# Delta-rule scan: longer gaps between some of its steps, a tile taken later, and the output projection begun beside the last scan but one

## The chip, the cores and the metric

The kernel runs on one core of a Trainium2 chip. The metric is the device time of one execution in microseconds (us). The core has a matrix engine (TensorE, PE in the profile), a vector engine (VectorE, DVE), a scalar engine (ScalarE, ACT), GpSimd (POOL) and a queue for transfers (SyncE, SP). Each takes its own instructions in order, and they wait for one another by semaphores.

## The reference

Two layers over 768 tokens (512 of one group, 256 of another) with 1024 features: a Fourier-style layer, then a bidirectional gated delta rule; each is followed by a SwiGLU mixer. The change lies in the second layer's mixer, which for 8 heads of width 128 computes:

```python
def gdn_mixer(h, w_in, conv_w, a_log, dt_bias, norm_g, w_out):
    proj = h @ w_in
    qkv = jax.nn.silu(centred_depthwise_conv(proj[..., :GDN_QKV_DIM], conv_w))
    z = proj[..., GDN_QKV_DIM:GDN_QKV_DIM + GDN_V_DIM]
    ...
    q = l2norm(q) * (GDN_HEAD_DIM ** -0.5)
    k = l2norm(k)
    ...
    o_fwd = gated_delta_chunked(q, k, v, g[:, :, 0], beta[:, :, 0])
    o_bwd = gated_delta_chunked(q[:, ::-1], ..., g[:, ::-1, 1], beta[:, ::-1, 1])[:, ::-1]
    o = o_fwd + o_bwd
    o = o * lax.rsqrt(jnp.mean(o * o, axis=-1, keepdims=True) + EPS) * norm_g * jax.nn.silu(z)
    return o.reshape(bsz, s, GDN_V_DIM) @ w_out
```

Within a chunk the rule needs the inverse of a unit triangular matrix; between chunks a state is carried on.

## The kernel before

Data lie feature by token. The 768 tokens are two segments (512 and 256) for long products and six chunks of 128 for the delta rule. A long product is made of split operands, a high and a low half each: per k-step and segment three matmuls, hh with wh, hl with wh, hh with wl (`passes`, all recorded at L128; the output is a PSUM bank named pr).

For each head, `prepare(h)` issues four such projections of eight k-steps: k, q, v and z. The first three pass through `conv_block` (conv on VectorE, L948, silu with L886 on VectorE and three steps on ScalarE). Beside the projections stand the steps of the delta rule, by a planner: every k-step calls `tick`, which moves a modelled clock, `line["now"]`, on and issues each step that is due, right behind that k-step (`run_next`). PLACES are the due times of the preparing steps (norm of k, products of k and q, transposes of v) after the head's base; SCAN is that of the start of `scan(h)`, which so stands beside the projections of head h + 1; HOPS are the gaps between the steps of the scan, which is a generator that yields the next gap. A Tile scheduler then orders each engine's instructions; what it decides is shown below by rows of the built programs.

`solve` (L1054 to L1071) inverts blocks of 16 by a chain of small VectorE steps between two passes through DRAM and yields cc. `invert` doubles the blocks at levels 16, 32 and 64: r (a masked cc, one half on POOL, one on VectorE, L1088), then transposes `ident,cc` (L1095), masked to t (VectorE, L1097), products `t,am` (am is the level's part of the matrix, masked on POOL), copied to t again (ScalarE, L1109; called zz here), products `r,t`, subtracted from cc (VectorE, L1119) or, at the last level, copied into rr (ScalarE, L1122, L1123). Four steps of the scan proper follow, over both directions at once: `st,kT`, xx (VectorE, L1155), `xx,rr` (`vk,rr` in the first), yk and yy (ScalarE), `yk,kk`, st (VectorE, L1172).

The scan's end: products `pm,yy` and `qd,st`, copied to ob (ScalarE, L1186); two squares on ScalarE (L1191, L1192), summed on POOL (L1193); a hop; products `yy,ones`; logarithm and exponential (L1199, L1200), two VectorE steps (L1201, L1202), and the head's gated output goes to DRAM (ogd, SP, L1204). The buffer rr of `invert` is also the one that L1196 takes at the scan's end.

The output projection reads heads 0 to 6 back from ogd into two buffers "wa" in turn (SP, L1216) and splits each into hh (ScalarE, L195) and hl (VectorE, L196), which overwrite the operands of the projections. Seven blocks of it run beside the last scan, number 7; block 7 and head 7's part come after. `residual` (VectorE, L473) adds a block to x. The products have three PSUM banks: two for segments of 512 (pr0) and one for 256 (pr1).

Of the kernel before, what the change touches and what calls it, by code (L numbers as in the profile page):

```python
# [12 lines left out]
F32 = mybir.dt.float32  # L13
# [7 lines left out]
P = 128  # L21
# [27 lines left out]
LANES = NT * P // BASE  # L49
LSTEP = BASE * (P + 1)  # L50
NEGBIG = -1e30
HOPS = (1150.0, 1300.0, 1500.0, 1400.0, 1300.0, 2080.0, 1150.0, 2700.0)
PLACES = (16100.0, 20200.0, 22900.0, 29400.0, 36200.0)
SCAN = 34100.0

_TAB = {}

# [48 lines left out]
def encoder_kernel(  # L106
# [53 lines left out]
    def load_block(w2d, k0, kc, m0):  # L160
        stg = fetch(w2d, k0, kc, m0)
        ah, al = [], []
        step = kc if kc <= HK else (kc + 1) // 2
        for a in range(0, kc, step):
            n = min(step, kc - a)
            wh, wl = split_w(stg[:, a : a + n])
            ah += [wh[:, k] for k in range(n)]
            al += [wl[:, k] for k in range(n)]
        return ah, al
# [612 lines left out]
    with ExitStack() as gs:  # L782
# [16 lines left out]
        def work(name="wa", bufs=2):  # L799
            return ga.tile([P, T + 2], F32, name=name, bufs=bufs)  # L800
# [99 lines left out]
        def run_next():  # L900
            t, _, fn = heapq.heappop(line["due"])
            with tc.issue_after(line["ins"]):
                fn()
# [175 lines left out]
        def invert(src):  # L1079

            cc = src["cc"]
            rr = gp.tile([P, 2, NT, P], F32, name="rr")
            halves = range(0, NT, NB)
            for lv in LEVELS:
                am = src["am"]
                r2 = gp.tile([P, NT, P], F32, name="r2")
                for b0 in halves:
                    (G if b0 in R2G else V).tensor_tensor(r2[:, b0 : b0 + NB], cc[:, b0 : b0 + NB], mask(f"B{lv}", NB), ALU.mult)  # L1088
                if lv != LEVELS[0]:
                    yield HOPS[0]  # L1090
                t1 = {}
                for b0 in halves:
                    pt = psm.tile([P, 512], F32, name="sm")
                    for i in range(NB):
                        nc.tensor.transpose(pt[:, i * P : (i + 1) * P], cc[:, b0 + i], ident)  # L1095
                    t1[b0] = gp.tile([P, NB, P], F32, name="t1", bufs=3)
                    V.tensor_tensor(t1[b0], tiles6(pt[:, : NB * P]), mask(f"A{lv}", NB), ALU.mult)  # L1097
                if lv == LEVELS[-1]:
                    for d in range(2):
                        G.affine_select(rr[:, d], cc, pattern=[[0, NT], [1 - 2 * d, P]], compare_op=ALU.is_ge, fill=0.0,  # L1100
                                        base=0, channel_multiplier=2 * d - 1)
                yield HOPS[1]
                zz = {}
                for b0 in halves:
                    pt = psm.tile([P, 512], F32, name="sm")
                    for i in range(NB):
                        mm(pt[:, i * P : (i + 1) * P], am[:, b0 + i], t1[b0][:, i])
                    zz[b0] = gp.tile([P, NB, P], F32, name="t1", bufs=3)
                    A_.copy(zz[b0], tiles6(pt[:, : NB * P]))  # L1109
                if lv != LEVELS[-1]:  # L1110
                    siblings(src, 2 * lv)
                yield HOPS[2]
                for b0 in halves:
                    cm = cc[:, b0 : b0 + NB]
                    pt = psm.tile([P, 512], F32, name="sm")
                    for i in range(NB):
                        mm(pt[:, i * P : (i + 1) * P], zz[b0][:, i], r2[:, b0 + i])
                    if lv != LEVELS[-1]:
                        V.tensor_tensor(cm, cm, tiles6(pt[:, : NB * P]), ALU.subtract)  # L1119
                    else:  # L1120
                        hp = P // 2
                        A_.copy(rr[:hp, 0, b0 : b0 + NB, hp:], tiles6(pt[:hp, : NB * P])[:, :, hp:])  # L1122
                        A_.copy(rr[hp:, 1, b0 : b0 + NB, :hp], tiles6(pt[hp:, : NB * P])[:, :, :hp])  # L1123
            return rr

        def scan(h, src):
# [11 lines left out]
            for stp in range(4):  # L1138
# [17 lines left out]
                    xin = lambda i: xx[:, i]  # L1156
                else:
                    xin = lambda i: vk[:, live[i][1]]
                yield HOPS[4]
                py = group(lambda d, j: rr[:, d, j], xin, len(live))  # L1160
                yk = gp.tile([P, 4, P], F32, name="yk") if more else None
                for i, (d, j) in enumerate(live[:more]):
# [46 lines left out]
        for h in range(H):  # L1209
            prepare(h)  # L1210

        while H - 2 not in scanned:
            run_next()
        for h in range(H - 1):
            ob = work()[:, :T]
            nc.sync.dma_start(ob, ogd[h])  # L1216
            split_to(hh[h], hl[h], ob)

        xs = [ga.tile(pad_shape, F32, name="pad"), *(ga.tile(head_shape, F32, name=n, bufs=b) for n, b in (("qT", 2), ("vT", 1))),
              work("we"), work("we"), work(), work()]  # L1220
        xs = [x[:, :T] for x in xs]
        for m in range(KC - 1):
            nc.sync.dma_start(xs[m], xd[m])
            po = product(ppr, load_block(gdn_w_out[0], 0, H - 1, m * P), hh, hl, H - 1, tick)
            residual(xs[m], po, GATE[2], m)
        drain()
# [123 lines left out]
```

## Time and profile before

| what | value |
|---|---|
| runs shown | 2956.52, 1903.44, 1901.87 us, median 1903.44 |
| profiled execution | 1905.38 us |
| its span, first to last instruction | 1903.7 us |
| mean granted TensorE clock | 0.989 |
| stretch of the six scans beside whole projections | 853 to 1233 us |
| the last head's projections, output projection, last scan | 1233 to 1345 us |

A wait in the profile is idle time of an engine ahead of an instruction, put down to what released it. In rows of the timeline the first column is the start in us from the span's start, the second the duration, and the bracket at the end the idle time with its releaser. In rows of stretches the columns are the busy times of the engines in it, then the granted clock, the share of the DMA engines, and GB/s. In groups by line the last columns are the busy time in us and the mean in ns, then idle time ahead.

### The profile page before, as it was taken

What the parts mean: (1) busy time and instruction counts of PE and PEld (TensorE: products, weight loads), DVE (VectorE), ACT (ScalarE), POOL (GpSimd) and SP (SyncE); (2) the same over time, 40 slices, a digit from 0 to 9 for tenths busy, and PEclk for the clock granted to TensorE, in tenths of its full rate; (3) what the DMA queues carried; (4) which work ended last, traced back from release to release, by engine and by line L of the source; (5) the groups of instructions that cost most, each with busy time, mean ns of one, the idle gap of its engine ahead of it and who ended that gap; (6) DMA issues with size and microseconds to landing.
All of it is one profiled execution on the core that took longest, in us unless ns stands there. A gap on an engine that the chain in (4) does not pass through costs nothing. (4 is left out here: it accounts for less than half of the span.)

```text
span 1903.7 us, 29939 instructions
## 1 busy us (share of the span) xinstructions
PE 1800.2 (95%) x11305; PEld 1641.0 (86%) x11305; DVE 1419.6 (75%) x2415; ACT 974.5 (51%) x1860; POOL 539.8 (28%) x436
## 2 busy tenths in 40 slices
PE   7898999999999998999999999989889999999998
PEld 6587889999999986888888888778789999999997
DVE  4636777767786777897787787783768888889875
ACT  3625544444454535856566556642654554555543
POOL 1403132333333320123213212321343334443431
PEclk9999999999999999999999999999999999999999
DMA  8742344343434354322212222141203222222211
GB/s 272 242 171 67 111 132 130 109 140 112 154 111 155 111 160 142 115 51 64 65 53 65 68 64 57 57 151 41 77 23 89 77 79 67 67 67 80 77 45 67
DMA packets 221546, 189.72 MB, mean 100 GB/s; under 512 B 19152, under 2 KB 199513, under 8 KB 221401
## 3 DMA queue, kind: packets, MB, share of 16 engines
q1 hardware_dynamic: 220992, 187.66, 32.2%
q8 instruction: 89, 1.46, 0.3%
q14 instruction: 56, 0.46, 0.1%
q10 hardware_dynamic: 409, 0.15, 0.0%
HBM read 174.36 MB, written 13.42 MB: 99 GB/s over the span
## 5 line engine op out<-in xcount | busy, mean ns | idle before, releaser
L128 PE MATMUL pr<-hh,wh 128*128 128x384 f32 (+2 forms) x1520 | 520.7, 346 | 15.0 <-ACT cs__676 L736 5.6
L128 PE MATMUL pr<-hl,wh 128*128 128x384 f32 (+2 forms) x1520 | 519.0, 342 | 6.9 <-DVE hl L196 6.6
L128 PE MATMUL pr<-hh,wl 128*128 128x384 f32 (+2 forms) x1520 | 517.8, 341 | 1.0 <-DVE wl L148 1.0
L147 ACT CAST wh<-stg 128x512 fp32r<-128x512 f32 (+1 forms) x376 | 226.2, 609 | 369.8 <-PE pr L128 254.5
L148 DVE TENSOR_TENSOR wl<-stg,wh 128x512 fp32r<-128x512 f32 (+1 forms) x376 | 290.9, 779 | 108.4 <-ACT wh L147 107.3
L128 PEld LDWEIGHTS pr<-hh,wh 128*128 128x128 f32 x1520 | 286.2, 189 | 39.2 <-ACT cs__676 L736 6.1
L128 PEld LDWEIGHTS pr<-hl,wh 128*128 128x128 f32 x1520 | 287.5, 189 | 25.6 <-DVE hl L196 8.6
L128 PEld LDWEIGHTS pr<-hh,wl 128*128 128x128 f32 x1520 | 286.8, 189 | 18.4 <-DVE wl L148 1.8
L128 PE MATMUL pr<-g,wh 128*128 128x384 f32 (+2 forms) x1072 | 274.1, 337 | 8.7 <-DVE x L552 8.7
L128 PEld LDWEIGHTS pr<-g,wh 128*128 128x128 f32 x1072 | 192.7, 188 | 13.4 <-DVE x L552 11.6
L128 PE MATMUL pr<-eh,wh 128*128 128x384 f32 x536 | 184.2, 347 | 13.3 <-ACT eh L195 9.2
L128 PE MATMUL pr<-el,wh 128*128 128x384 f32 x536 | 182.6, 341 | 0.4 <-DVE el L196 0.4
L128 PE MATMUL pr<-eh,wl 128*128 128x384 f32 x536 | 182.5, 340 | 0.0
L128 PE MATMUL pr<-g,wl 128*128 128x384 f32 (+2 forms) x536 | 180.3, 336 | 0.0
L383 POOL TENSOR_TENSOR s<-stg 128x512 f32<-128x512 f32 x42 | 60.1, 1432 | 402.2 <-DMA stg<-in_ffn_w_gu_dram 360.8
L128 PEld LDWEIGHTS pr<-eh,wh 128*128 128x128 f32 x536 | 102.5, 192 | 22.4 <-ACT eh L195 10.1
L517 DVE TENSOR_TENSOR wl<-stg,wh 128x512 fp32r<-128x512 f32 x108 | 88.2, 818 | 34.1 <-ACT wh L516 33.3
L948 DVE SCALAR_TENSOR_TENSOR wa<-pad,cwT,wa 128x770 f32<-128x770 f32 x96 | 108.9, 1134 | 4.6 <-ACT wa L945 3.3
L516 ACT CAST wh<-stg 128x512 fp32r<-128x512 f32 x108 | 66.9, 621 | 80.5 <-PE pr L128 63.2
L128 PEld LDWEIGHTS pr<-el,wh 128*128 128x128 f32 x536 | 102.3, 191 | 1.4 <-DVE el L196 1.3
L128 PEld LDWEIGHTS pr<-eh,wl 128*128 128x128 f32 x536 | 102.3, 191 | 0.0
L128 PEld LDWEIGHTS pr<-g,wl 128*128 128x128 f32 x536 | 100.6, 188 | 0.7
(370 smaller groups left out, 3172.9 us busy)
## 6 DMA issues: line engine op xcount, KB each, us to landing
stg<-in_ffn_w_gu_dram SPq DMA_DIRECT2D x88, 512.0 KB, 4.1
stg<-in_ada_w_dram SPq DMA_DIRECT2D x56, 512.0 KB, 5.0
at<-in_ada_w_dram SPq DMA_DIRECT2D x40, 512.0 KB, 4.8
stg<-in_ffn_w_down_dram SPq DMA_DIRECT2D x36, 512.0 KB, 3.7
stg<-in_gdn_w_in_dram SPq DMA_DIRECT2D x33, 512.0 KB, 4.2
stg<-in_final_ada_w_dram SPq DMA_DIRECT2D x16, 512.0 KB, 6.1
raw<-gcd SPq DMA_DIRECT2D x8, 768.0 KB, 4.0
stg<-in_fnet_w_dram SPq DMA_DIRECT2D x8, 512.0 KB, 7.7
```

The source lines that it names most:

```text
L128: return nc.tensor.matmul(out, lhsT, rhs, start=start, stop=stop, **kw)
L147: A_.copy(wh[:, :n], src)
L148: V.tensor_tensor(wl[:, :n], src, wh[:, :n].bitcast(F32), ALU.subtract)
L383: eng.tensor_tensor(out, a, b, op)
L516: A_.copy(wh, src)
L517: V.tensor_tensor(wl, src, wh.bitcast(F32), ALU.subtract)
L948: V.scalar_tensor_tensor(acc, pad[:, d : d + T + 2], wc[d], acc, ALU.mult, ALU.add)
```

## The change

Six edits. HOPS[0], ahead of the transposes of levels 32 and 64, goes from 1150 to 1950 modelled ns. A new entry of 1900 takes the place of HOPS[4], 1300, in the first of the four steps. HOPS[7], ahead of `yy,ones`, goes from 2700 to 4500. SCAN goes from 34100 to 35000. So a scan starts 0.9 modelled us later and its gaps are 4.0 longer in sum (34.2 in place of 30.2; a head's projections are 31.0). The tile rr of `invert` is taken at level 64, where it is first written, instead of at the start.

The output projection is written anew: the two weight blocks 0 and 1 are loaded first, heads 0 to 5 are read back and split, and three jobs, block 0's two segments and block 1's first, each with a bank of its own, go on together, k-step by k-step, through heads 0 to 5 (`onward`). Only then is the rest of scan 6 run, with the modelled clock set to the due time of each step; head 6 is read back; the three jobs take their last k-step; and block 1's second segment and the blocks 2 to 6 follow as before. The inputs of the residuals are loaded in another order.

```diff
--- before.py
+++ after.py
@@ -49,9 +49,9 @@
 LANES = NT * P // BASE
 LSTEP = BASE * (P + 1)
 NEGBIG = -1e30
-HOPS = (1150.0, 1300.0, 1500.0, 1400.0, 1300.0, 2080.0, 1150.0, 2700.0)
+HOPS = (1950.0, 1300.0, 1500.0, 1400.0, 1300.0, 2080.0, 1150.0, 4500.0, 1900.0)
 PLACES = (16100.0, 20200.0, 22900.0, 29400.0, 36200.0)
-SCAN = 34100.0
+SCAN = 35000.0
 
 _TAB = {}
 
@@ -1079,7 +1079,6 @@
         def invert(src):
 
             cc = src["cc"]
-            rr = gp.tile([P, 2, NT, P], F32, name="rr")
             halves = range(0, NT, NB)
             for lv in LEVELS:
                 am = src["am"]
@@ -1096,6 +1095,7 @@
                     t1[b0] = gp.tile([P, NB, P], F32, name="t1", bufs=3)
                     V.tensor_tensor(t1[b0], tiles6(pt[:, : NB * P]), mask(f"A{lv}", NB), ALU.mult)
                 if lv == LEVELS[-1]:
+                    rr = gp.tile([P, 2, NT, P], F32, name="rr")
                     for d in range(2):
                         G.affine_select(rr[:, d], cc, pattern=[[0, NT], [1 - 2 * d, P]], compare_op=ALU.is_ge, fill=0.0,
                                         base=0, channel_multiplier=2 * d - 1)
@@ -1156,7 +1156,7 @@
                     xin = lambda i: xx[:, i]
                 else:
                     xin = lambda i: vk[:, live[i][1]]
-                yield HOPS[4]
+                yield HOPS[4 if stp else 8]
                 py = group(lambda d, j: rr[:, d, j], xin, len(live))
                 yk = gp.tile([P, 4, P], F32, name="yk") if more else None
                 for i, (d, j) in enumerate(live[:more]):
@@ -1209,18 +1209,46 @@
         for h in range(H):
             prepare(h)
 
-        while H - 2 not in scanned:
-            run_next()
-        for h in range(H - 1):
+        def gated(h):
             ob = work()[:, :T]
             nc.sync.dma_start(ob, ogd[h])
             split_to(hh[h], hl[h], ob)
 
-        xs = [ga.tile(pad_shape, F32, name="pad"), *(ga.tile(head_shape, F32, name=n, bufs=b) for n, b in (("qT", 2), ("vT", 1))),
-              work("we"), work("we"), work(), work()]
-        xs = [x[:, :T] for x in xs]
-        for m in range(KC - 1):
-            nc.sync.dma_start(xs[m], xd[m])
+        w01 = [load_block(gdn_w_out[0], 0, H - 1, m * P) for m in range(2)]
+        for h in range(H - 2):
+            gated(h)
+
+        def back(t):
+            xs.append(t[:, :T])
+            nc.sync.dma_start(xs[-1], xd[len(xs) - 1])
+
+        xs = []
+        back(ga.tile(pad_shape, F32, name="pad"))
+        back(work("we"))
+        jobs = [(bank(ppr, g), w01[m], *SEGS[g]) for m, g in ((0, 0), (0, 1), (1, 0))]
+        ready = [passes(ps, w, [a[:, lo : lo + ln] for a in hh[: H - 1]], [a[:, lo : lo + ln] for a in hl[: H - 1]],
+                        skip_group_check=True) for ps, w, lo, ln in jobs]
+
+        def onward():
+            for (_, _, _, ln), gen in zip(jobs, ready):
+                tick(ln * 3 * 0.421, next(gen))
+
+        for h in range(H - 2):
+            onward()
+        while H - 2 not in scanned:
+            line["now"] = max(line["now"], line["due"][0][0])
+            run_next()
+        gated(H - 2)
+        for t in (work("we"), *(ga.tile(head_shape, F32, name=n, bufs=b) for n, b in (("qT", 2), ("vT", 1))), work(), work()):
+            back(t)
+        onward()
+        residual(xs[0], [jobs[0][0], jobs[1][0]], GATE[2], 0)
+        lo, ln = SEGS[1]
+        ps = bank(ppr, 1)
+        for last in passes(ps, w01[1], [a[:, lo : lo + ln] for a in hh[: H - 1]], [a[:, lo : lo + ln] for a in hl[: H - 1]]):
+            tick(ln * 3 * 0.421, last)
+        residual(xs[1], [jobs[2][0], ps], GATE[2], 1)
+        for m in range(2, KC - 1):
             po = product(ppr, load_block(gdn_w_out[0], 0, H - 1, m * P), hh, hl, H - 1, tick)
             residual(xs[m], po, GATE[2], m)
         drain()
```

In the rows that follow, lines of the changed kernel from L1082 to L1095 are one less than those of the same statement before (L1094 there is L1095 here).

The first place is a steady head, here the one whose scan runs beside head 7's projections, on TensorE, from the last products of a level to the transposes of the next. Before:

```order
L128 MATMUL sm<-t_11784,am 128x128 x3
L128 MATMUL pr_11924<-hl_80,wh 128x512
L128 MATMUL sm<-r_11707,t_11810 128x128 x3
L128 MATMUL pr_11924<-hh_72,wl 128x512
L128 MATMUL sm<-r_11707,t_11816 128x128 x3
L128 MATMUL pr_11924<-hh_73,wh 128x512
L128 MATMUL pr_11924<-hl_81,wh 128x512
L128 MATMUL pr_11924<-hh_73,wl 128x512
L128 MATMUL pr_11924<-hh_74,wh 128x512
L1095 MATMUL sm<-ident,cc 128x128 x3
```

After, at the same place:

```order
L128 MATMUL sm<-r_11682,t_11807 128x128 x3
L128 MATMUL sm<-r_11682,t_11813 128x128 x3
L128 MATMUL sm<-yy,ones 128x512
L128 MATMUL ax<-wa,ones 128x512
L128 MATMUL sm<-yy,ones 128x256
L1094 MATMUL sm<-ident,cc 128x128 x6
L128 MATMUL ax<-wa,ones 128x256
L128 MATMUL sm<-t_11905,am 128x128 x3
L128 MATMUL sm<-t_11911,am 128x128 x3
L128 MATMUL pr_11897<-hh_77,wl 128x512
```

The projection's matmuls that stood singly between products and transposes are gone from here, and the norm products of the scan before (`yy,ones`) and of k (`ax<-wa,ones`) stand in their place.

The same place on VectorE, from the subtractions of level 32 to the masks of level 64. Before:

```order
L1119 TENSOR_TENSOR cc<-cc,sm 128x384
L1202 TENSOR_TENSOR zs<-ob,zs 128x768
L1119 TENSOR_TENSOR cc<-cc,sm 128x384
L1088 TENSOR_TENSOR r_11839<-cc,gtab 128x384
L1097 TENSOR_TENSOR t_11856<-sm,gtab 128x384
L1097 TENSOR_TENSOR t_11862<-sm,gtab 128x384
```

After, at the same place:

```order
L1119 TENSOR_TENSOR cc<-cc,sm 128x384 x2
L1087 TENSOR_TENSOR r_11840<-cc,gtab 128x384
L886 TENSOR_SCALAR we<-wa 128x770
L1096 TENSOR_TENSOR t_11905<-sm,gtab 128x384
L1096 TENSOR_TENSOR t_11911<-sm,gtab 128x384
L1201 SCALAR_TENSOR_TENSOR ob<-ob,gT,rr 128x768
```

L886, the first step of a silu, has come between r and the masks, and the step L1201 of the scan's end, which stood ahead of the subtractions, now follows the masks.

The second place is the begin of the output projection on TensorE; hh_71 to hh_78 and hl_79 to hl_86 are the halves of heads 0 to 7. Before, from its first product:

```order
L128 MATMUL pr_12318<-hh_71,wh 128x512
L128 MATMUL pr_12429<-hh_71,wh 128x512
L128 MATMUL pr_12356<-hh_71,wh 128x256
L128 MATMUL sm<-st,kT 128x128 x2
L128 MATMUL pr_12318<-hl_79,wh 128x512
L128 MATMUL pr_12318<-hh_71,wl 128x512
L128 MATMUL pr_12318<-hh_72,wh 128x512
L128 MATMUL sm<-xx,rr 128x128
L128 MATMUL sm<-pm,yy 128x128
L128 MATMUL sm<-xx,rr 128x128
L128 MATMUL sm<-qd,st 128x128 x2
L128 MATMUL pr_12356<-hl_79,wh 128x256
```

After, at the same place:

```order
L128 MATMUL pr_12252<-hh_71,wh 128x512
L128 MATMUL pr_12254<-hh_71,wh 128x512
L128 MATMUL pr_12253<-hh_71,wh 128x256
L128 MATMUL pr_12252<-hl_79,wh 128x512
L128 MATMUL pr_12252<-hh_71,wl 128x512
L128 MATMUL pr_12253<-hl_79,wh 128x256
L128 MATMUL pr_12253<-hh_71,wl 128x256
L128 MATMUL pr_12254<-hl_79,wh 128x512
L128 MATMUL pr_12254<-hh_71,wl 128x512
L128 MATMUL sm<-st,kT 128x128 x2
L128 MATMUL pr_12252<-hh_72,wh 128x512
L128 MATMUL pr_12252<-hl_80,wh 128x512
```

The three unfinished products go through a head together, and the scan's last products (`pm,yy`, `qd,st`) no longer stand among those of the first heads.

VectorE at that place. Before, from the state's update to the split of head 1:

```order
L1066 TENSOR_TENSOR rl<-rl,tmp 48x2x7x9
L1172 SCALAR_TENSOR_TENSOR st<-st,tot,sm 128x128
L1065 TENSOR_TENSOR tmp<-rl,uu 48x128
L196 TENSOR_TENSOR hl_79<-wa,hh_71 128x768
L1066 TENSOR_TENSOR rl<-rl,tmp 48x2x8x8
L1155 SCALAR_TENSOR_TENSOR xx<-sm,neg,vk 128x128
L1065 TENSOR_TENSOR tmp<-rl,uu 48x126
L1155 SCALAR_TENSOR_TENSOR xx<-sm,neg,vk 128x128
L1066 TENSOR_TENSOR rl<-rl,tmp 48x2x9x7
L1047 TENSOR_TENSOR zs<-we,zs 128x768
L1065 TENSOR_TENSOR tmp<-rl,uu 48x120
L196 TENSOR_TENSOR hl_80<-wa,hh_72 128x768
```

After, at the same place:

```order
L1172 SCALAR_TENSOR_TENSOR st<-st,tot,sm 128x128
L1065 TENSOR_TENSOR tmp<-rl,uu 48x128
L886 TENSOR_SCALAR we<-zs 128x768
L1066 TENSOR_TENSOR rl<-rl,tmp 48x2x8x8
L196 TENSOR_TENSOR hl_79<-wa,hh_71 128x768
L1065 TENSOR_TENSOR tmp<-rl,uu 48x126
L196 TENSOR_TENSOR hl_80<-wa,hh_72 128x768
L1066 TENSOR_TENSOR rl<-rl,tmp 48x2x9x7
L1065 TENSOR_TENSOR tmp<-rl,uu 48x120
```

L886 of z's silu has moved behind the state's update and ahead of the first split, and the second split follows the first after one step.

The third place is the end of scan 6 on TensorE. Before:

```order
L128 MATMUL sm<-yy,ones 128x512
L128 MATMUL sm<-yy,ones 128x256
L128 MATMUL pr_12318<-hh_74,wh 128x512
L128 MATMUL pr_12318<-hl_82,wh 128x512
L128 MATMUL pr_12318<-hh_74,wl 128x512
L128 MATMUL pr_12318<-hh_75,wh 128x512
L128 MATMUL pr_12318<-hl_83,wh 128x512
L128 MATMUL pr_12318<-hh_75,wl 128x512
```

After, with the products of scan 7's level 32 ahead:

```order
L128 MATMUL sm<-t_12394,am 128x128 x3
L128 MATMUL sm<-t_12400,am 128x128 x3
L128 MATMUL sm<-r_12371,t_12435 128x128 x3
L128 MATMUL sm<-r_12371,t_12441 128x128 x3
L128 MATMUL sm<-yy,ones 128x512
L128 MATMUL sm<-yy,ones 128x256
L128 MATMUL pr_12252<-hh_77,wh 128x512
L128 MATMUL pr_12253<-hh_77,wh 128x256
L128 MATMUL pr_12252<-hl_85,wh 128x512
L128 MATMUL pr_12252<-hh_77,wl 128x512
L1094 MATMUL sm<-ident,cc 128x128 x6
```

Before, products of heads 3 and 4 (hh_74, hh_75) follow the norm products; after, those of head 6 (hh_77) do, and heads 0 to 5 are all ahead.

On ScalarE at that place. Before, from the copies of ob:

```order
L1186 COPY ob<-sm 128x384 x2
L1191 ACTIVATE yy<-qT 128x768
L1192 ACTIVATE yy<-ob 128x768
L195 CAST hh_74<-wa 128x768
L195 CAST hh_75<-wa 128x768
L985 COPY vk<-ax 128x384 x2
L1199 ACTIVATE rr<-sm,epsq 128x512
L1199 ACTIVATE rr<-sm,epsq 128x256
L1200 ACTIVATE rr<-rr 128x768
```

After, at the same place:

```order
L1186 COPY ob<-sm 128x384 x2
L1191 ACTIVATE yy<-qT 128x768
L1192 ACTIVATE yy<-ob 128x768
L1109 COPY t_12435<-sm 128x384
L1109 COPY t_12441<-sm 128x384
L1199 ACTIVATE rr<-sm,epsq 128x512
L1199 ACTIVATE rr<-sm,epsq 128x256
L1200 ACTIVATE rr<-rr 128x768
```

The two copies L1109 of scan 7's level 32 now stand between the squares and the norm's logarithms, and no split of a head stands there.

## The prediction

> **What bounds the kernel now.** I read the page first, then TensorE's waits by stretch, then the timeline around the two places where the change reorders most.
>
> ```profile
> span 1903.7 us, 29939 instructions
> PE 1800.2 (95%) x11305; PEld 1641.0 (86%) x11305; DVE 1419.6 (75%) x2415; ACT 974.5 (51%) x1860; POOL 539.8 (28%) x436
> ```
>
> TensorE is busy 95% of the span, and the change removes no matmul: all it can move is TensorE's waits. The profiled run took 1905.38 us, 1.7 more than its span; the median of the runs shown is 1903.44, so a sum against the span is one against the median too. What the change touches lies in the delta-rule stage. First the waits of six scans (853 to 1233 us; columns: total us, times, longest), in which a scan's steps stand between the next head's projections:
>
> ```profile
> PE sm L128 <- POOL yy L1193: 5.2, 4, 1.3
> PE sm L1095 <- DVE cc L1119: 4.6, 6, 1.2
> PE sm L1095 <- DMA cc<-solved: 3.7, 4, 1.2
> PE sm L128 <- POOL wa L946: 3.4, 2, 1.7
> PE sm L128 <- ACT rr L1123: 1.6, 4, 0.6
> PE sm L1095 <- ACT ob L1186: 1.3, 3, 0.7
> PE sm L128 <- ACT rr L1122: 0.4, 2, 0.2
> ```
>
> The norm products (yy,ones) wait 5.2 + 3.4, the transposes (L1095) for the corrected inverse 4.6 + 1.3, the first step's products 1.6 + 0.4: 16.5 us that longer hops address, and 3.7 us of a DMA (cc) that they don't. Now the stretch from the end of head 7's projections to the arrival of head 6's output, where the order of the output projection changes:
>
> ```profile
> PE sm L128 <- DVE st L1172: 1.4, 1, 1.4
> PE sm L128 <- POOL yy L1193: 1.3, 1, 1.3
> PE pr L128 <- DVE hl L196: 0.6, 1, 0.6
> PE sm L128 <- DVE t L1097: 0.3, 1, 0.3
> ```
>
> Only 3.6 us wait there, because three unfinished products stand between everything else. The timeline gives what a wait costs beside its idle time:
>
> ```profile
> 1253.74 0.51 PE L128 MATMUL pr<-hl,wh 128*128 128x512 f32 x1 [0.58 <-DVE hl L196]
> 1254.09 0.39 PE L128 MATMUL pr<-hh,wl 128*128 128x512 f32 x1
> 1254.32 0.40 PE L128 MATMUL pr<-hh,wh 128*128 128x512 f32 x1
> ```
>
> After the wait the next matmul starts 0.35 us later, undisturbed ones 0.23 apart: a wait costs some 0.12 us beyond the bracket. The 0.23 also prices the output projection: a k-step of the three jobs is 15 units of 0.117 (two matmul triples of 512 columns, one of 256), 1.75 us.
>
> **The steady scans.** The hops move the yy,ones products, the transposes and the first step some 0.6 to 1.8 modelled us later, which by the order puts them behind whole groups of other matmuls. The 16.5 us go, and with 21 waits at 0.12 another 2.5: -19.0. What comes is of three kinds.
>
> First, the solve chain. A head's inverse starts with DMAs and a row of VectorE steps, and TensorE meets its end:
>
> ```profile
> 1166.19 0.61 PE L128 MATMUL ax<-kT 128*128 128x128 f32 x4
> 1170.18 0.36 SPq L1017 DMA_DIRECT2D atd<-at  x1
> 1190.76 0.33 SPq L1069 DMA_DIRECT2D solved<-uu  x1
> 1192.83 0.36 SPq L1071 DMA_DIRECT2D cc<-solved  x1
> 1197.14 0.87 PE L1095 MATMUL sm<-ident,cc 128*128 128x128 f32 x6 [1.22 <-DMA cc<-solved]
> ```
>
> 31.0 us from ax<-kT to the transposes, 1.22 of it waiting. Before, such long waits alternate with heads where more matmuls lie between and almost nothing is left (3.7 us in 4 times); by the order every head after has the shorter cover, so I take 6 x 1.1 = 6.6 in place of 3.7: +2.9 (0 to 6). The later start of a scan, 0.9 modelled us, does not help here, as no more matmuls stand ahead of its first transposes than in those heads.
>
> Second, the masks of level 64 (t on VectorE). By the order L886 of the next silu now stands ahead of them, while POOL forms its half of r (L1088):
>
> ```profile
> L886 DVE TENSOR_SCALAR we<-wa x14: 550/565/2064, 906.1 to 1195.8; 128x770 f32<-128x770 f32 x14
> 1208.28 1.81 POOL L1193 TENSOR_TENSOR yy<-yy 128x768 f32<-128x768 f32 x1
> 1208.80 1.83 DVE L148 TENSOR_TENSOR wl<-stg,wh 128x512 fp32r<-128x512 f32 x1 [0.43 <-ACT wh L147]
> ```
>
> L886 takes 0.55 us alone (lowest, median and highest in ns): 6 x 0.5 = +3.0 on the products t,am, with bounds of 0 (TensorE comes late anyway) and 1.2 each, +7, since the highest, 2.06, and the stretched L148 show VectorE held up beside POOL. [...]
>
> Third, zz (L1109) of level 32 stands on ScalarE behind both squares of the scan's end. A group of 47 projection matmuls stands between there, 7.5 modelled us, so only +1.0 for stragglers (0 to 3). The tile rr is taken late because the scan's end, which uses the same buffer, now follows the next inverse's begin; POOL's selects wait for L1201, but 30 projection matmuls, some 5 us, stand between yy,ones and the products whose result goes into rr: 0. Steady sum: -19.0 + 2.9 + 3.0 + 1.0 = **-12.1**, bounds -19 and -3 (all late at once, +16).
>
> **The transition.** Here the jobs of the output projection use heads 0 to 5 ahead of scan 6's end. All three banks belong to the jobs, so TensorE, in order, has nothing else when a job lacks its head. Head 0's first product comes here:
>
> ```profile
> 1249.75 1.09 PE L128 MATMUL pr<-hh,wh 128*128 128x512 f32 x3
> ```
>
> The second half hl came 4.0 us later (1253.74 above). In the new order hl stands behind L886 (0.55, itself after the copy of z) and a 0.95 us subtraction: 2.8 us after the projections' end, 0.6 of it covered: 2.1. Then each reload goes through two buffers. From the rows below, a reload costs 3.6 us from issue to its cast, 0.83 for the cast and 0.95 for hl, and the next but one may be issued only then: 5.4 us per two heads, or 2.7 per head against 1.75 of matmuls and short scan steps. Heads 2 to 5 and the step xx add about 3.5 us. Last, cc of head 7 is loaded behind these reloads on SP's queue and its solve steps stand between the hl's on VectorE: +1.2 more. 6.8 together (3 to 9). The two levels of scan 7 and scan 6's last steps then follow each other without any product between them: masks +0.8 (0 to 1.5). There the two squares delay zz:
>
> ```profile
> L1109 ACT COPY t<-sm 128x384 f32<-128x384 f32 x28 | 13.5, 482 | 34.0 <-PE sm L128 34.0
> L1191 ACT ACTIVATE yy<-qT 128x768 f32<-128x768 f32 x5 | 4.2, 850 | 0.0
> L1192 ACT ACTIVATE yy<-ob 128x768 f32<-128x768 f32 x5 | 4.2, 838 | 0.0
> ```
>
> r,t waits for a copy of ob, two squares and zz, 0.48 + 0.85 + 0.84 + 0.48 = 2.65, less 0.66 of t,am: 2.1, and yy,ones 0.7 more for POOL's sum (2.8; 2 to 3.4). The largest term is the round trip of head 6's output, which before was hidden:
>
> ```profile
> 1264.08 1.56 PE L128 MATMUL sm<-yy,ones 128*128 128x512 f32 x4 [1.29 <-POOL yy L1193]
> 1265.24 1.05 ACT L1199 ACTIVATE rr<-sm,epsq 128x512 f32<-128x512 f32 x2 [0.61 <-PE sm L128]
> 1267.21 1.02 DVE L1201 SCALAR_TENSOR_TENSOR ob<-ob,gT,rr 128x768 f32<-128x768 f32 x1 [1.50 <-ACT rr L1200]
> 1268.75 0.95 DVE L1202 TENSOR_TENSOR zs<-ob,zs 128x768 f32<-128x768 f32 x1
> 1269.72 0.32 SPq L1204 DMA_DIRECT2D ogd<-zs  x1
> 1272.09 0.32 SPq L1216 DMA_DIRECT2D wa<-ogd  x1
> 1275.73 0.83 ACT L195 CAST hh<-wa 128x768 fp32r<-128x768 f32 x1 [1.04 <-DMA wa<-ogd]
> 1277.72 0.95 DVE L196 TENSOR_TENSOR hl<-wa,hh 128x768 fp32r<-128x768 f32 x1
> ```
>
> From the products' start to the end of the cast: 1276.56 - 1264.08 = 12.5 us, about 0.6 of it a step of VectorE that stood between. After, the products' 1.2 us are followed at once by pr<-hh_77, head 6's: 11.9 - 1.2 = 10.7 us stand open, and 0.7 for hl: 11.4 (10 to 12). A gap of that length also costs clock:
>
> ```profile
> 1368.66 0.69 PE L128 MATMUL pr<-eh,wh 128*128 128x384 f32 x1 [4.27 <-ACT eh L195]
> 1368.00:1376.00 8.00, 7.34 (x33) 7.11 (x34) 8.00 (x14) 8.00 (x17) 0.00 (x0) 0.79 0.00 0
> 1399.90 0.69 PE L128 MATMUL pr<-hl,wh 128*128 128x384 f32 x1 [3.48 <-DVE hl L196]
> 1399.80:1410.00 10.20, 10.10 (x41) 9.87 (x42) 7.86 (x15) 4.86 (x10) 1.01 (x1) 0.70 0.08 24
> ```
>
> Behind gaps of 4.27 and 3.48 us the granted clock (the figure ahead of the last two) is 0.79 over 8.0 us and 0.70 over 10.2: 8.0 x 0.21 = 1.7 and 10.2 x 0.30 = 3.1 us. I take 2.4 (0 to 3.1). [...]
>
> Come: 6.8 + 0.8 + 2.8 + 11.4 + 2.4 = 24.2; gone: the 3.6 us above and four times 0.12, 4.1. Transition **+20.1**, bounds +11 (3 + 0 + 2 + 10 + 0 less 4.1) and +25. At nothing I cost the moved residual inputs, whose loads follow the reloads and are used 10 us later, the two weight blocks loaded early (three loads of them stood ahead of the same reloads on SP before, and do so after), and the later end of scan 7, which by the planner's hops still lies well within the remaining output projection.
>
> **Sum:** 1903.7 - 12.1 + 20.1 = 1911.7, say **1911**.
>
> **The rivals.**
> - *The waits go and little follows* (the faster side): steady scans at -19, transition at +11: 1903.7 - 8 = 1896. For it: the new hops target the largest waits one by one. Against: the order shows no matmul between yy,ones and head 6's product, so the 10 us are certain but for the DMA's own spread. It decides against me when the transition costs less than the scans give. Chance 0.27.
> - *The solve chain becomes the bound* (slower): the hops push more of a scan onto VectorE's queue among the solve's serial steps. Every microsecond by which cc comes later than 1.1 is paid in each of six scans; at 1.9 more, the 12 us gained are lost, and the time is 1911.7 + 11.4 = 1923. For it: 1.22 of wait already, with no slack. Against: the number of VectorE steps is the same. From 1.2 more per scan on, the time is above my forecast's own range below. Chance 0.18.
> - *The order hardly changes*, as hops are earliest places only: 1904. Against it speaks the order of both kernels, which differs in each head. Chance 0.05.
>
> **How the numbers follow.** My forecast holds 0.50. Its own range is 1904 to 1919 (either part off by 7). With the rivals, 1895 to 1921 holds all of the last, nearly all of the first and a part of the second, leaving out about 0.2. A measurement of this kernel tells a change from none at about 2%, 38 us: for slower by that, cc would have to come some 6 us later than forecast in each scan (0.02); for faster, more waits would have to go than the stretch has (0.01). Same: 0.97.
>
> **What would show it.** In TensorE's waits of the six scans, yy, cc L1119 and rr should be nearly gone, the DMA cc<-solved at 6 or 7 us, t (masks) at about 3. In the transition a single wait of pr for ACT's hh of 10 to 11 us, with a granted clock under 1 behind it, several waits of pr for hh and hl of 0.3 to 2 before it, and r,t waiting about 2 us for t L1109. If head 6's wait is under 8 us, a cover exists that I did not see in the order; if the scans' waits keep their size, the hops were not what set them.

## The result, and the profile after

The changed kernel took 1920.11 us in the median of 4 runs, the kernel before 1905.72 beside it: ratio 1.0075, 95% interval 1.0055 to 1.0094, some 14 us slower. One of the four runs before took 2956.52 us; without it their median is 1903.44, and the difference is 17 us. The forecast was 1911 us, range 1895 to 1921. The page of the changed kernel shows as many matmuls, 4.7 us more busy time of TensorE and, in a span longer by 15.2 us, 10.5 us more waiting:

```profile
span 1918.9 us, 29921 instructions
PE 1804.9 (94%) x11305; PEld 1643.8 (86%) x11305; DVE 1421.9 (74%) x2415; ACT 976.2 (51%) x1860; POOL 540.8 (28%) x436
```

TensorE's waits in the same stretch of six scans, 853 to 1233 us (columns: total us, times, longest). Two rows of before that the prediction does not list:

```profile
PE ax L128 <- DVE kT L1012: 1.2, 2, 0.7
PE sm L128 <- DVE t L1097: 1.2, 2, 0.6
```

After:

```profile
PE sm L128 <- DVE t L1096: 6.9, 9, 1.0
PE ax L128 <- DVE kT L1012: 5.3, 5, 1.1
PE sm L1094 <- DMA cc<-solved: 3.1, 4, 1.0
PE sm L1094 <- DVE cc L1119: 2.6, 6, 0.5
PE sm L128 <- DVE cc L1119: 1.9, 6, 0.4
PE sm L128 <- DVE st L1172: 0.9, 4, 0.2
PE sm L128 <- POOL yy L1193: 0.4, 1, 0.4
```

The 16.5 us that the hops addressed (yy, wa, cc L1119, ob, rr) are down to 3.0. In their place VectorE is waited for, under names that had been small or absent: the masks t, the normalized k (kT), and PSUM banks that the subtraction L1119 has to free (sm <- DVE cc L1119). The rows sum to 21.1 us; all rows of before summed to 22.8.

And the transition, from 1233 to 1360 us:

```profile
PE pr L128 <- ACT hh L195: 12.0, 3, 9.7
PE pr L128 <- DVE hl L196: 2.1, 1, 2.1
PE sm L1094 <- DMA cc<-solved: 1.9, 1, 1.9
PE sm L128 <- DVE xx L1155: 1.2, 1, 1.2
PE sm L128 <- POOL yy L1193: 1.1, 1, 1.1
PE sm L128 <- ACT t L1109: 1.1, 1, 1.1
```

One wait of 9.7 us carries it. Its timeline, from the norm products of scan 6 to head 6's first product, and the granted clock around it (columns of the two last rows: stretch, its length, busy times of PE, PEld, DVE, ACT and POOL, clock, DMA share, GB/s):

```profile
1284.11 1.56 PE L128 MATMUL sm<-yy,ones 128*128 128x512 f32 x4 [1.11 <-POOL yy L1193]
1289.27 0.32 SPq L1204 DMA_DIRECT2D ogd<-zs  x1
1291.62 0.32 SPq L1214 DMA_DIRECT2D wa<-ogd  x1
1294.51 0.83 ACT L195 CAST hh<-wa 128x768 fp32r<-128x768 f32 x1 [7.31 <-DMA wa<-ogd]
1295.39 1.01 PE L128 MATMUL pr<-hh,wh 128*128 128x512 f32 x2 [9.73 <-ACT hh L195]
1284.50:1290.00 5.50, 1.17 (x4) 0.38 (x2) 1.98 (x2) 1.90 (x3) 2.50 (x3) 0.79 0.00 0
1290.00:1300.00 10.00, 4.61 (x15) 3.63 (x16) 3.25 (x6) 1.34 (x2) 0.78 (x1) 0.50 0.45 157
```

Head 6 goes to DRAM and back, and TensorE has nothing else in its queue; then 1.01 us for two matmuls that take some 0.63 in a row at full clock (0.40 each, starting 0.23 apart). In this trace the clock is 0.50 from 1287.68 to 1301.33 us, and TensorE worked 5.94 us of it.

To divide the time, four points serve that every kernel has: the first ax<-kT of head 0, of head 2 and of head 7, and the first product of the mixer that follows (pr<-eh). They are starts in the timeline; the last row goes on to the end of the last matmul; the time up to the first of them differs between profiled executions (783 to 792 us) although nothing is changed there, so spans alone do not compare parts of a few us.

| us | before | after | difference |
|---|---|---|---|
| ax<-kT, head 0 to head 2 | 108.03 | 104.51 | -3.5 |
| ax<-kT, head 2 to head 7 | 338.85 | 339.97 | +1.1 |
| ax<-kT of head 7 to pr<-eh | 135.73 | 151.68 | +16.0 |
| pr<-eh to the end of the last matmul | 527.74 | 528.33 | +0.6 |

So the six scans gave 2.4 us, all of it beside the first heads, and the transition took 16. In the transition TensorE's idle time rose from 12.8 to 25.7 us and its busy time from 122.9 to 126.0, about what 5.94 us at half clock add. Seven kernels, the changed one and six of those below, have the same six scans; they took 339.8 to 340.3 us from head 2 to head 7, so that part repeats within half a us; the mixer behind pr<-eh, which no run changes, took 524.2 to 528.4.

### The profile page after: what moved, and what is told of

It reads as the page before. It is cut to its first block, busy times and chain, and to the rows that moved or that the text cites. A ratio compares the mean times of both kernels' runs of the same rounds, so it can differ in the third digit from the quotient of the medians.

```text
span 1918.9 us, 29921 instructions
## 1 busy us (share of the span) xinstructions
PE 1804.9 (94%) x11305; PEld 1643.8 (86%) x11305; DVE 1421.9 (74%) x2415; ACT 976.2 (51%) x1860; POOL 540.8 (28%) x436
## 5 line engine op out<-in xcount | busy, mean ns | idle before, releaser
L148 DVE TENSOR_TENSOR wl<-stg,wh 128x512 fp32r<-128x512 f32 (+1 forms) x376 | 284.8, 764 | 131.5 <-ACT wh L147 130.4
L128 PEld LDWEIGHTS pr<-hh,wh 128*128 128x128 f32 x1520 | 286.9, 189 | 51.0 <-ACT hh L195 13.2
L948 DVE SCALAR_TENSOR_TENSOR wa<-pad,cwT,wa 128x770 f32<-128x770 f32 x96 | 116.0, 1208 | 4.6 <-ACT wa L945 3.3
```

The lines of the kernel that those rows point to most:

```text
L128: return nc.tensor.matmul(out, lhsT, rhs, start=start, stop=stop, **kw)
L148: V.tensor_tensor(wl[:, :n], src, wh[:, :n].bitcast(F32), ALU.subtract)
L948: V.scalar_tensor_tensor(acc, pad[:, d : d + T + 2], wc[d], acc, ALU.mult, ALU.add)
```

## Experiments: the transition

Each measurement starts with the time as a ratio to the kernel before, run beside it, with its 95% interval. "The stretch" is that from head 7's first ax<-kT to pr<-eh.

Theory A was that the hops did it: by due times scan 6's last steps come behind scan 7's first, and so behind head 7's late cc. Theory B was that the rewritten projection did it, with three jobs in lockstep on all banks.

**New hops, old projection.** Only the projection's part is taken back:

```diff
+        while H - 2 not in scanned:
+            line["now"] = max(line["now"], line["due"][0][0])
+            run_next()
+        for h in range(H - 1):
+            ob = work()[:, :T]
...
-        w01 = [load_block(gdn_w_out[0], 0, H - 1, m * P) for m in range(2)]
```

> New hops, later start and late rr, with the old output projection (scan 6's rest still run by due times, as the changed kernel does it). Two theories of the 16 us that the change adds behind head 7's projections. Theory A: the hops. Their sum, 34.2 modelled us, is longer than a head, 31.0, so by due times scan 6's last steps stand behind scan 7's first transposes, and those wait for the solve's cc; head 6's output then comes too late, whatever the projection looks like. Theory B: the rewritten projection. Three jobs in lockstep use heads 0 to 5 up and hold all banks, so nothing is left for the round trip of head 6. A expects 8 to 16 us more than before, with a wait of pr for hh of 5 us or more, and cc<-solved in the transition at 2 us or more; B expects within 3 us of before and no such wait. Both expect the six steady scans as in the changed kernel: head 7's first ax<-kT 1 to 2 us earlier than before.

Measured: 1.0048 of before (1.0029 to 1.0066); from head 7's ax<-kT to pr<-eh 146.18 us, 10.5 more than before. The wait of pr for hh is there, in the same view of this kernel's stretch from 1239 to 1345 us:

```profile
PE pr L128 <- ACT hh L195: 8.5, 3, 5.5
```

No wait for cc shows in that stretch, though theory A expected one of 2 us or more. The old projection does not save it, so B alone falls.

**Old hops, new projection.** The kernel before with the new out-projection.

> Old hops, old start and early rr, with the new output projection. Its joint k-steps move the modelled clock by 9.7 us, so scan 7's start falls due ahead of scan 6's last step here too. Theory A (scan 6's end behind scan 7's begin) expects 8 to 14 us more than before, with cc<-solved waiting 2 us or more ahead of the round trip; theory B (lockstep and banks) 13 to 17 us more with a wait of pr for hh of 9 to 10 us. Were the hops alone to blame, it would be within 3 us of before. The six steady scans are those of before, within 1 us.

Measured: 1.0088 (1.0063 to 1.0114); 153.66 us for the stretch, 17.9 more than before, and the steady heads as before (338.68 from head 2 to 7). Stretch 1235 to 1345 us:

```profile
PE pr L128 <- ACT hh L195: 12.6, 3, 10.5
PE sm L1095 <- DMA cc<-solved: 1.9, 1, 1.9
```

The hops alone are not needed either. Either part by itself costs most of the 16 us, and the two do not add.

**Scan 6 first.** In both forms, scan 6's remaining steps are taken from the planner's heap ahead of anything else:

```diff
+        def finish_scan(h):
+            while h not in scanned:
+                due = min(d for d in line["due"] if getattr(d[2], "head", None) == h)
+                line["due"].remove(due)
+                heapq.heapify(line["due"])
+                with tc.issue_after(line["ins"]):
+                    due[2]()
...
-        while H - 2 not in scanned:
...
+        finish_scan(H - 2)
```

With the old projection:

> As the first (new hops, old output projection), but scan 6's remaining steps are all issued ahead of scan 7's first. Theory A expects the transition as before: within 4 us of before in all, the steady gain of 1 to 2 us in it, and the wait of pr for hh under 5 us. If the solve of head 7 or the reloads themselves set the end, it stays 8 us or more above before.

Measured: 1.0047 (1.0032 to 1.0062), the stretch 146.48 us: nothing gained on the first run of this section. With the new one, scan 6 also ahead of the jobs' k-steps:

> The changed kernel, but scan 6's remaining steps are issued ahead of the jobs' k-steps and of scan 7's first. Theory A expects 0 to 8 us more than before, at least 7 less than the changed kernel, since scan 6 no longer waits for cc; theory B, that the lockstep with all banks held costs it, 12 to 17 us more than before, as in the changed kernel.

Measured: 1.0041 (1.0024 to 1.0058), 146.44 us, 5.2 less than the changed kernel. In both the wait for head 6 stays, the first of these rows from the kernel with the old projection (1239 to 1360 us), the second with the new one (1230 to 1350 us):

```profile
PE pr L128 <- ACT hh L195: 6.1, 2, 5.8
PE pr L128 <- ACT hh L195: 6.4, 2, 4.9
```

With the old projection the waits for hh are 2.4 us shorter than in the first run, but a wait for a weight block's split has come that the first run does not have:

```profile
PE pr L128 <- ACT wh L147: 4.0, 1, 4.0
```

Theory A fell short: the order of the two scans is worth 5 us of the 16 with the new projection and in sum none with the old.

**Head 6 without the way through DRAM.** What all four seem to have in common is that little work stands between scan 6's end and head 6's product. So the way itself was cut: head 7's projections are done by then and head 6's operands free.

```diff
-            if h < H - 1:
+            if h < H - 2:
                 nc.sync.dma_start(ogd[h], zs)
...
-        gated(H - 2)
```

> The changed kernel, but head 6's gated output is split straight into its operands, without the way through DRAM (head 7's projections are done by then, so the operands are free). If the round trip of head 6 is what stands open, the wait of pr for ACT's hh, 9.7 us, falls to 3 to 4.5, and the time is 5 to 8 us below the changed kernel's (some 1 us of it from the clock). Rival: scan 7's transposes, which wait for head 7's cc and follow in the same order, take the place as the bound; then it is within 2 us of the changed kernel.

Measured: 1.0049 (1.0033 to 1.0065), by the ratios 5 us under the changed kernel, and 5.5 less in the stretch (146.18); the longest wait of pr for hh went from 9.7 to 4.5. So the way through DRAM is paid nearly one for one; it is 5.2 of the 9.7 us. The other 4.5 are the chain that stays: logarithm, exponential, two VectorE steps and the split.

**Three edits together**: scan 6 first, head 6 direct, and a priority for k's normalization (below).

> The changed kernel with scan 6's steps ahead of the jobs and of scan 7, head 6's output split directly, and the normalization of k given priority. If the three causes are separate, 11 to 16 us come off the changed kernel's time: from 4 below before to 2 above it. If they share one bound (scan 7's cc), 6 to 9 come off, and it stays 6 us or more above before.

Measured: 1.0006 (0.9996 to 1.0017); the stretch took 138.49 us, 13.2 less than in the changed kernel. Without the priority:

> The changed kernel with scan 6's steps ahead of the jobs and of scan 7, and head 6's output split directly, without the priority for k's normalization that moved waits only. The transition should be as in the run with three edits, 138 to 139 us from head 7's first ax<-kT to the next layer part, 13 less than changed, and the steady heads as in the changed kernel: 1 us below to 1 us above before.

Measured: 1.002 (1.0009 to 1.0032), 139.66 us. The two edits together take off 12.0 us, where each alone took off 5 to 6: they are separate costs. It stays 4 us above before; in the transition the waits are now spread (yy L1202 2.9, hh 1.9, wh 1.9).

**Filler in the gap.** For the clock, 36 matmuls whose result nobody reads were put behind scan 6's norm products:

```diff
+        with tc.issue_after(line["norm"].ins):
+            warm = psm.tile([P, 512], F32, name="sm")
+            for i in range(36):
+                mm(warm, w01[0][0][0], hh[0][:, :512])
         gated(H - 2)
```

> The changed kernel, with 36 extra matmuls (128x512, result unused, 8.4 us by their pitch) behind the norm products of scan 6, where TensorE waits for head 6. If the half clock behind that wait costs 2.4 us, the granted clock from 1290 to 1300 us is above 0.9 and the time 1 to 3 us below the changed kernel's. Rival: the work behind the wait is bound by other engines, so the clock costs nothing: within 1 us. If the extra matmuls held head 6 back, 1 us more or above.

Measured: 1.0079 (1.0061 to 1.0097), the stretch 153.20 us, 1.5 more than changed. The filler ran from 1286.99 to 1295.72, 1.77 us stayed open ahead of head 6's first product at 1297.49, and the clock from 1290 to 1300 us was 0.97. The 1.5 us do not come from the filler. TensorE has the same order of instructions in both kernels from head 7's first ax<-kT (1231.68 and 1231.71) to yy,ones, yet this one starts yy,ones, ahead of the filler, at 1285.79 in place of 1284.11, because in its profiled execution two pieces of that stretch ran at half clock. First one of them in the changed kernel, then three pieces of the kernel with the filler (columns as above):

```profile
1251.64:1255.05 3.41, 3.41 (x22) 2.96 (x22) 3.32 (x10) 1.19 (x2) 0.00 (x0) 1.00 1.04 367
1251.64:1255.05 3.41, 3.41 (x12) 2.92 (x12) 2.83 (x7) 1.23 (x2) 0.00 (x0) 0.50 1.01 335
1296.01:1299.42 3.41, 1.79 (x9) 1.27 (x10) 1.80 (x3) 1.20 (x2) 0.00 (x0) 1.00 0.21 84
1299.42:1302.84 3.42, 3.42 (x13) 2.93 (x12) 3.14 (x6) 0.51 (x1) 0.00 (x0) 0.50 0.42 124
```

The half clock behind head 6's first product came all the same, only later and shorter (1299.42 to 1302.84, in place of 1287.68 to 1301.33); from that product to pr<-eh it took 87.42 us against 87.97. In all TensorE worked 9.9 us at half clock in this stretch and 5.9 in the changed kernel. So this run doesn't settle what the clock costs. It shows another thing: one piece of half clock, 3.41 us, held 12 matmuls in place of 22 and costs up to an estimated 1.7 us, half its length (yy,ones came 1.68 us later behind two), and where it falls differs between executions with the same order. Differences of 1 to 2 us between single profiled transitions (138.4 and 139.7, or 151.5 and 153.2) are no proof of an edit's effect.

## Experiments: the six scans

**k's normalization first.**

```diff
-                V.tensor_tensor(kT, kT, rs, ALU.mult)
+                with tc.high_priority():
+                    V.tensor_tensor(kT, kT, rs, ALU.mult)
```

> The changed kernel, with the normalization of k (L1012 on VectorE) given priority, so that it stands ahead of the two weight splits L148 (1.15 us) that it now stands behind. If that queue makes ax<-kT wait in the steady heads, its waits, 5.3 us in the six scans, fall under 1.5 and the time is 4 to 6 us below the changed kernel's. Rival: the exponential on ScalarE ahead of it (L962) is what comes late, delayed by the norm of the scan's end that now stands at the same place; then 3.5 us or more of the wait stay and the time is within 2 us.

Measured: 1.0085 (1.0066 to 1.0103). Head 2 to 7 took 340.78 us against 339.97, head 0 to 2 106.40 against 104.51. From head 2 to 7 (890.6 to 1231.4 us) the wait is as it was, and another one has come:

```profile
PE sm L128 <- DVE t L1097: 7.5, 9, 1.0
PE ax L128 <- DVE kT L1013: 5.3, 6, 1.0
PE sm L128 <- DVE xx L1156: 3.7, 4, 0.9
```

The rival's numbers came, but neither cause was right: the two L148 did go behind, and the exponential was not the bound either. From 1159.89 the exponential ran to 1160.73 and then the product qd (1.76 us) stood ahead of L1013 until 1162.57. VectorE's queue is full there; passing one instruction only showed the next.

**HOPS[7] back at 2700**, the only edit:

> The changed kernel with only HOPS[7] back at 2700. By the order the norm products of a scan then stand ahead of the last products of level 32, not among the norm of the next k and behind those. If the new waits of the steady heads come from these two norms and the level meeting at one place, the waits for kT (5.3 us) and for the banks that cc L1119 frees (PE sm L128, 1.9 us) shrink to under 3 in sum, and from head 2's to head 7's first ax<-kT it takes 336 us or less in place of 340.0. Rival: VectorE is simply full there, so that what stands early for one is late for another: 339 to 341 again, with the transposes' wait for cc L1119 or the masks' t grown instead. The transition stays as in the changed kernel within 3 us in both.

Measured: 1.007 (1.0053 to 1.0086); head 2 to 7 in 337.36 us, 2.6 less than changed and 1.5 less than before. But head 0 to 2 took 107.76 us, 3.3 more than changed, so that from head 0 to 7 nothing is gained (445.12 us, changed 444.48). The waits from head 2 to 7 (893.9 to 1231.25 us):

```profile
PE sm L128 <- DVE t L1096: 8.1, 13, 0.8
PE sm L128 <- POOL yy L1193: 4.5, 5, 0.9
PE sm L1094 <- DMA cc<-solved: 2.2, 4, 0.9
PE sm L128 <- DVE xx L1155: 2.2, 2, 1.2
PE sm L1094 <- DVE cc L1119: 2.2, 5, 0.4
```

kT and the banks are gone, as the first theory has it; but yy is back, t has grown, and the stretch lies between the two forecasts. So the meeting of the two norms makes these two waits, and the rival has the larger part: what one wait loses another finds. VectorE shows why t did not shrink. L886 has left the place behind r and takes 0.56 us now, but L1201 stands there in its stead, beside GpSimd's half of r, in each of five heads. In this kernel, then in the changed one, where nothing of GpSimd runs beside it (shortest, median, longest in ns):

```profile
L1201 DVE SCALAR_TENSOR_TENSOR ob<-ob,gT,rr x5: 1567/1571/1578, 953.2 to 1222.6; 128x768 f32<-128x768 f32 x5
L1201 DVE SCALAR_TENSOR_TENSOR ob<-ob,gT,rr x5: 1017/1018/1019, 954.7 to 1223.6; 128x768 f32<-128x768 f32 x5
```

With the two edits of the transition:

> The same with HOPS[7] back at 2700. If the steady heads gain by it (first theory of the run before), 3 to 5 us below before; by the rival, within 2 us of before.

Measured: 1.0002 (0.999 to 1.0015), 138.43 us for the transition and 337.38 for head 2 to 7, but 444.60 from head 0 to 7, as changed: the kernel is as fast as before, 14 us faster than the changed one by the ratios. Of the 3 us by which it lies under the two edits alone, the parts show 1.2 in the transition and none in the scans, so that HOPS[7] as their cause is not shown. None of the kernels run was faster than before beyond its interval.

**No work on GpSimd beside the masks.** Both halves of r on VectorE:

```diff
-R2G = (3,)
+R2G = ()
```

> The changed kernel with both halves of r on VectorE, so that GpSimd does nothing beside L886 ahead of the masks of level 64. If L886's 1.36 us there (0.55 alone) is GpSimd's half of r holding it up, its median falls to 0.55 to 0.6, VectorE takes 1.65 us between the subtractions and the masks in place of 1.91, and the waits of the products for the masks t, 5.5 us from head 2 to head 7, fall to 3.5 or less; the stretch then takes 337.5 to 339.5 us in place of 340.0. Rival: L886 is long for another reason; it stays at 1.2 or more, the masks come half a us later, and the waits for t grow to 7 or more.

Measured: 1.005 (1.0034 to 1.0067), though the transition is as costly as in the changed kernel (151.54 us): head 2 to 7 took 330.83 us, 9.1 less, and head 0 to 2 as in the changed kernel (104.50). By the ratios the whole gains only 5 us; the profiled execution, 1909.33 us, was the fastest of four, of which the others took 1912 to 1915. First L886 in the three kernels, before, changed and this one (shortest, median, longest in ns), over the six scans:

```profile
L886 DVE TENSOR_SCALAR we<-wa x15: 550/565/2064, 906.1 to 1226.1; 128x770 f32<-128x770 f32 x15
L886 DVE TENSOR_SCALAR we<-wa x15: 548/1362/1374, 904.6 to 1220.6; 128x770 f32<-128x770 f32 x15
L886 DVE TENSOR_SCALAR we<-wa x16: 549/564/1375, 900.2 to 1228.5; 128x770 f32<-128x770 f32 x16
```

The median hides two places. Of the 15 in the changed kernel five stand beside GpSimd's r and five beside another GpSimd product, am (L1077, 1.81 us). The five beside r fell from 1.36 to 0.55 us; the five beside am stay at 1.37. Then the place itself in the changed kernel's timeline:

```profile
1220.14 0.55 DVE L1087 TENSOR_TENSOR r<-cc,gtab 128x384 f32<-128x384 f32 x1
1220.37 1.18 POOL L1087 TENSOR_TENSOR r<-cc,gtab 128x384 f32<-128x384 f32 x1 [2.95 <-DVE cc L1119]
1220.61 1.36 DVE L886 TENSOR_SCALAR we<-wa 128x770 f32<-128x770 f32 x1
1221.89 1.01 DVE L1096 TENSOR_TENSOR t<-sm,gtab 128x384 f32<-128x384 f32 x2
1222.58 1.58 PE L128 MATMUL sm<-t,am 128*128 128x128 f32 x12 [0.98 <-DVE t L1096]
```

GpSimd's r ends at 1221.55 and L886, begun at 1220.61, 0.42 us later. Without GpSimd's half, the waits of head 2 to 7 (891.34 to 1222.17 us) are:

```profile
PE sm L1094 <- DMA cc<-solved: 3.1, 4, 1.0
PE sm L128 <- DVE st L1172: 2.9, 6, 0.5
PE sm L1094 <- DVE cc L1119: 2.2, 5, 0.4
PE sm L128 <- POOL yy L1193: 1.9, 5, 0.4
PE sm L128 <- DVE cc L1119: 0.8, 5, 0.2
```

No row of t, none of kT. The gain is larger than expected (0.5 to 2.5 us), because a shorter queue on VectorE relieved kT too. It is not L886's 0.81 us less alone: with the other durations the scheduler also put both norm products of k, 512 and 256 columns, between the transposes and t,am, where only the 256 stood.

This edit together with the two of the transition was not run, nor on the kernel before. If the parts add, the form with two edits, 4 us above before (1.002), would come out 1 us below it with the 5 us by the ratios off, and some 5 below with the 9 of the profile; that is an estimate, and whether GpSimd's half of r cost anything in the order of before stays open.

## Why the forecast came out as it did

The sign was right, and the number lay 9 us under the measured one. Two errors of opposite sign make 5.6 of it: the scans gave 9.7 us less than forecast, and the transition cost 4.1 less. The rest is in parts that the change does not touch and in the base, which was 1903.7 in the sum and 1905.72 in the result. That the time lies in the range, by 1 us, is owed in part to luck: it is outside the forecast's own 1904 to 1919, and with the transition as dear as forecast it would have passed 1921.

- *What goes from the scans, -19.0:* held for the most part. The addressed rows fell from 16.5 to 3.0 us, 7 waits in place of 21.
- *What comes, +6.9:* failed. The step was the second kind, "6 x 0.5 = +3.0 on the products t,am", and the missing kinds. t rose by 5.7 us instead of 3.0 and lay inside its bounds; kT rose by 4.1 and the banks by 1.9, neither of which the sum had. Behind t and kT stands in large part what the forecast priced as an instruction of 0.55 us with some delay: the VectorE instruction beside GpSimd's half of r, L886 at 1.36 us, in the middle of a full VectorE queue. With that half on VectorE both rows are gone; as the order on TensorE moved too, the share of each is not shown. L886 took 1.36 us beside r and 0.55 without GpSimd's half; priced at that 1.36 in the five heads where it stood there, the term would have been an estimated 6.8 in place of 3.0, and the sum nearer. The third kind, zz at +1.0, has no row. The steady sum was -12.1 forecast, -2.4 measured from head 0 to head 7, outside the bounds of -19 to -3 by little.
- *The solve chain, +2.9:* did not come. cc<-solved waits 3.1 us against 3.7 before; the wait of a head never passed 1.0. The rival that lived on it is gone too.
- *The reloads and cc, 6.8:* hl 2.1, then hh 1.4 and 0.8, zs 0.3 and cc 1.9 make 6.5. Held.
- *Masks between the levels, 0.8, and the squares, 2.8:* no wait for masks, 1.1 for t L1109 and 1.1 for yy. 1.4 us too high together: the working took 0.66 us for t,am, whose twelve passes took 1.50 (from 1278.82), so that more of the squares was covered.
- *The round trip, 11.4:* 9.7, and no wait for hl behind it, since the two matmuls ahead took 1.01 us at half clock. From yy,ones to the end of the cast 1295.34 - 1284.11 = 11.2 us; the forecast had 11.9; the reload took 2.9 us from issue to cast (1291.62 to 1294.51) and not 3.6. The run without DRAM shows 5.2 us of it to be the way through memory; 4.5 are the chain of norm and split.
- *The clock, 2.4:* TensorE worked 5.94 us at 0.50 behind the wait, from 1295.39 to 1301.33; half of that, an estimated 3.0 us, lies inside the bounds of 0 to 3.1. The size agrees, but the run that was to test it could not take it away.
- *Transition +20.1:* 16.0 measured, inside its bounds. What came, 6.5 + 2.2 + 9.7 + 3.0, is 21.4 us against 24.2; the rest of the difference is in small waits of before that are absent after.
- *rr taken late and the new order of the residual inputs, 0:* nothing in the waits names either; no run tests them alone.

## What to carry to other kernels

Gaps made longer so that products no longer wait moved the wait here to VectorE's queue (t by 5.7 us, kT by 4.1): before pricing an instruction that an order puts ahead of a waiting one, look at what runs beside it on another engine (L886 took 1.36 us beside GpSimd's r, 0.55 without it), and at everything behind it in that queue, not at its own 0.55 us. Work that is taken forward to fill a gap is work that will be missing at the next one; where the last producer's output comes back through memory, count what is left to do between its end and its first use (head 6's product waited 9.7 us here).

## What the runs showed of the hardware

- Beside a GpSimd product of 128x384 (1.18 us), a VectorE instruction of 0.55 us (L886) took 1.36, and another of 1.02 us (L1201) took 1.57 when the order put it in the same place (HOPS[7] back at 2700). With that product on VectorE (0.55 us), the profile has 9.1 us less in a stretch of 340, the ratios 5 us less in all.
- Half clock came in pieces of 3.41 us or whole multiples (6.83 us from 72.54 and 13.65 from 1287.68 in the changed kernel), and the length of a gap alone did not decide it. A gap of 2.13 us in the changed kernel (up to 1251.35) was followed by full clock, one of 2.17 us at the same place of the same order (up to 1251.40, kernel with the filler) by half clock. The 3.41 us ahead of two such pieces held 1.40 us of work (changed kernel, up to 1287.68) and 1.79 (kernel with the filler, up to 1299.42); the two such stretches over which the gap of 2.13 us fell (counted back from the half clock's begin at 1287.68), 2.21 and 2.20.
